# Two one-tile steps at the head of an input projection, and a load put behind the first scale pieces

## The chip, the cores and the metric

One core of a Trainium2 chip. The metric is the device time of one execution in microseconds (us), the median of the runs shown. PE (TensorE) multiplies, ACT (ScalarE) and DVE (VectorE) do elementwise work, POOL (GpSimd) and SP (SyncE) issue DMAs here.

## What is computed

One step of a hybrid decoder layer, float32, on 256 prompt positions and 8 samples (264 columns in all). What matters for this change is its head:

```python
mod = jax.nn.silu(c) @ p['w_mod'] + p['b_mod']          # w_mod: 2048 x 12288
sh_m, sc_m, gt_m, sh_f, sc_f, gt_f = split(mod, 6)
h = rmsnorm(x, p['g_mix']) * (1.0 + sc_m) + sh_m         # 2048 features
proj = h @ p['w_in']                                     # w_in: 2048 x 10256
...                                                      # three branches, gates, merge, w_out
h2 = rmsnorm(x, p['g_ffn']) * (1.0 + sc_f) + sh_f
x = x + gt_f * conv_ffn(h2)                              # 2048 x 11264, 5632 x 2048
```

To form a feature tile (128 features) of `h`, the kernel needs the root mean square of x over all features, and the scale (`sc_m`, section 1) and the shift (`sh_m`, section 0) of these features, each a sum over all 2048 inputs of `c`.

## The kernel before

Activations lie with features on the partitions, as 16 k tiles of 128 features by 264 columns. A weight W and an activation X are split into a high and a low part (`hi`, `lo`; `xh`, `xl`), and a product is three matmuls: hi·xh, hi·xl, lo·xh (`gemm_piece`). `load_w` brings a piece of a weight on SP's queue into one of three `raw` buffers; ACT copies it to `hi`, DVE subtracts to get `lo` (four buffers each). `prefetch` and `take` keep up to three pieces traced ahead of the one in use.

The first part of the input projection (12 column groups of 256 of the branches' inputs, 4 of gate b, and one of 128 for `dt`; 17 in all) runs in steps over k, since `h` becomes known k tile by k tile. `KSTEPS` lists them as (first k tile, number of tiles): (0,2), (2,2), (4,4), (8,4), (12,4). In each step all 17 groups are multiplied into PSUM (`PG`, three buffers) and read out: by ACT (a copy to `acc`) in step 0, by DVE (an addition to `acc`) in later ones. `cuts(s)` says which groups share a weight piece: 4 divided by the step's tiles, so pieces are 512 KB, some less at the cuts; `dt` is a piece of its own at the end.

The modulation of a step is computed by `mod_part` from pieces of 512 KB (128 x 1024, two per section and k tile), by `mod_load` into the seven buffers of `rm`; step 0's are issued on SP, all later ones on POOL. `mod_fin` copies the sums (`mev`, ACT), transposes them on TensorE (`modT`), adds four partial sums and the bias (DVE); then `modulate` (called by `step_h`) makes `ht`, `xh` and `xl`. `mod_gen` is the generator of a later step's modulation: it first issues loads, `depth` turns ahead, two pieces a turn, then consumes them. `mpump(n)` adds n to a credit and lets the generator run while it is at least 1; a turn costs 2 for steps of one or two tiles and 1 for four. Each group adds 0.8, or 0.4 where the next step has one tile. What is left when a step's groups end is run by `mfinish`, then `step_h`.

Before the first step, L1183 to L1233 load step 0's modulation (`load_first`), keep TensorE busy with products of zeros (`warm`), square x (`first_sq`), sum over features (`sum_tok`, TensorE) and form `rstd0` (`rstd_tok`, which ends in a product with `dg`).

A planner puts the instructions of each engine in order: among those that its own timing takes to be ready, the one traced first. `tc.high_priority()` moves a block ahead. `tc.issue_after(ins)` queues what the block traces on the engine of `ins` behind `ins`, in order of issue alone. Tiles get their buffers as they are released.

Of the kernel before, what the change touches and what calls it, by code (L numbers as in the profile page):

```python
# [13 lines left out]
AF = mybir.ActivationFunctionType  # L14
# [17 lines left out]
NFF = 44  # L32
NGA = 4
FFP = [(0, 24), (24, 20)]
KSTEPS = [(0, 2), (2, 2), (4, 4), (8, 4), (12, 4)]

# [27 lines left out]
def cuts(s):  # L66


    if s == len(KSTEPS) - 1:
        return [[g] for g in (8, 9, 10, 11, DT, 0, 1, 2, 3, 4, 5, 6, 7, *range(12, 12 + NGA))]  # L70
    n = 4 // KSTEPS[s][1]
    out = [[DT]]
# [5 lines left out]
def pack(i):  # L78
# [8 lines left out]
    wm = f("w_mod")[0]  # L87
    for s, (k0, nk) in enumerate(KSTEPS):
        w2 = wm[:, :4096].reshape(2 * nk, 8 // nk, P, 2, D)
# [10 lines left out]
    dtp[:, :16] = dt  # L100
    for s, (k0, nk) in enumerate(KSTEPS):
        r = slice(P * k0, P * (k0 + nk))
# [95 lines left out]
def build(tc, I, O):  # L198
    nc = tc.nc
    V, S, G, TE = nc.vector, nc.scalar, nc.gpsimd, nc.tensor  # L200
# [28 lines left out]
    def W(name, shape, dt=F32):  # L229
        return wp.tile(shape, dt, tag="w", name=nm(name))  # L230

    def PM(name):
        return pm.tile([P, 512], F32, tag="m", name=nm(name))

    def PG():
        return pg.tile([P, 2, 512], F32, tag="g", name=nm("pg"))
# [4 lines left out]
    def add(o, a, b, e=V):  # L241
        e.tensor_tensor(o, a, b, op=ALU.add)
# [13 lines left out]
    def act(o, a, f, **kw):  # L256
        S.activation(o, a, f, **kw)  # L257

    def mm(o, l, r, start, stop, **kw):
        TE.matmul(o, l, r, start=start, stop=stop, skip_group_check=True, **kw)  # L260

    def newest(e):

        return next(i for i in reversed(nc.cur_bb.bb.instructions) if i.engine == e.engine)


    ident = cst.tile([P, P], F32, name="ident")
# [8 lines left out]
    def pv(n, lo=0, hi=None):  # L276
        o, w = PAR_OFF[n]
        return par[:, o + lo:o + (w if hi is None else hi)]
# [25 lines left out]
    def prefetch(n=AHEAD):  # L304
        while queue and len(ahead) <= n:
            ahead.append(load_w(*queue.popleft()))
# [23 lines left out]
    mod_ps, mod_ev = {}, {}  # L330

    def mod_load(s_, nk, sec, i):

        raw = RM("rawm")
        (nc.gpsimd if s_ else nc.sync).dma_start(raw, I[f"w_m{s_}"][2 * nk * sec + i])
        return raw.rearrange("p (k n) -> p k n", k=8 // nk)

    def mod_part(sec, i, nk, raw):
        if sec not in mod_ps:
            mod_ps[sec] = PM("mod"), [0] * 4  # L340
        ps, seen = mod_ps[sec]
        for j in range(8 // nk):
            k = 8 // nk * i + j
            c = k % 4
            seen[c] += 1
            mm(ps[32 * c:32 * c + 32, :128 * nk], cs[:, k, :], raw[:, j, :], seen[c] == 1, seen[c] == KD // 4,
               tile_position=(0, 32 * c))

    def mod_fin(sec, k0, n):
        ps, _ = mod_ps.pop(sec)  # L350
        ev = W("mev", [P, 512])
        act(ev[:, :n], ps[:, :n], AF.Copy)
        mod_ev[0] = ev
        pt = PM("modT")
        nt = n // 128
        for t in range(nt):
            TE.transpose(pt[:, 128 * t:128 * t + 128], ev[:, 128 * t:128 * t + 128], ident)  # L357
        f = 16 * sec + k0
        m = mod[:, f:f + nt, :]
        V.tensor_reduce(m, pt[:, :n].rearrange("p (t g c) -> p t c g", t=nt, g=4)[:, :, :9, :],  # L360
                        axis=AX.X, op=ALU.add)
        add(m, m, pv("b_mod", f, f + nt).unsqueeze(2).to_broadcast([P, nt, 9]))
# [123 lines left out]
    def mpump(n):  # L486
        mcredit[0] += n
        while mods and mcredit[0] >= 1:
            try:
                mcredit[0] -= next(mods[0])  # L490
            except StopIteration:
                mods.popleft()
        if not mods:
            mcredit[0] = 0.0
# [9 lines left out]
    rstd0 = cst.tile([P, T], F32, name="rstd0")  # L504

    def sum_tok(pt, sqs, first, last):

        for i, sq in enumerate(sqs):
            for b, t0 in enumerate((0, 128, T - 128)):
                mm(pt[:, b:b + 1], sq[:, t0:t0 + 128], ones[:, :1], first and i == 0 and b == 0,  # L510
                   last and i == len(sqs) - 1)
        return pt
# [19 lines left out]
    def first_sq():  # L532
        sq = []
        for j in range(4):
            sq.append(Q("sq"))
            act(sq[j], x[j], AF.Square)
            if j:
                add(sq[0], sq[0], sq[j])
        h = sq[0][:, :2, :]
        add(h, h, sq[0][:, 2:, :])  # L540
        return [h[:, 0, :], h[:, 1, :]]
# [600 lines left out]

    for s_, (k0, nk) in enumerate(KSTEPS):
        o = 0
        for i, gs in enumerate(cuts(s_)):
            n = 128 if gs == [DT] else 256 * len(gs)
# [17 lines left out]
    def DEPTH(s_):  # L1164
        nk = KSTEPS[s_][1]
        return 4 * nk if s_ == 0 else (4, 4, 1)[nk // 2]

    def step_mods(s_):
        k0, nk = KSTEPS[s_]
        return mod_gen(s_, k0, nk, DEPTH(s_))  # L1170
# [10 lines left out]
    wps = PG()  # L1181
# [3 lines left out]
    def warm(n, src=None):  # L1185

        for _ in range(n):
            if src is None:
                mm(wps[:, 0, :256], wsrc[:, :128], wsrc, True, True)
            else:  # L1190
                mm(wps[:32, 0, :256], ident[:, :32], src, True, True)


    n0 = KSTEPS[0][1]
# [3 lines left out]
    def load_first(n):  # L1198
        for sec, i in first[len(got):len(got) + n]:
            got.append(mod_load(0, n0, sec, i))  # L1200

    load_first(3)
    nc.sync.dma_start(par[:, :NPAR1], I["par"][:, :NPAR1])
    load_first(3)
    pgm = lambda n: PG()[:, 0, :]
    sq0 = first_sq()
    warm(72)
    pt0 = None
    for n, (sec, i) in enumerate(first):
        if n == 0:  # L1210
            prefetch(0)
            load_first(1)
        if n == 1:
            load_first(1)
        if n == 3:
            rs0 = rstd_tok(pt0, pgm)
            scale = newest(S)
        mod_part(sec, i, n0, got[n])
        if i == 2 * n0 - 1:
            with tc.issue_after(scale), tc.high_priority():  # L1220
                if n == 3:
                    act(rstd0, rs0, AF.Copy)
                mod_fin(sec, KSTEPS[0][0], 128 * n0)
        if n == 2:
            pt0 = sum_tok(pgm("sst"), sq0, True, True)
        if n < 7:
            warm(5)
    warm(3, mod_ev[0][:, :256])
    step_h(0)
    with tc.issue_after(newest(S)), tc.issue_after(newest(V)):  # L1230
        prefetch(1)
# [3 lines left out]
    for s_, (k0, nk) in enumerate(KSTEPS):  # L1235
        nxt = None
        if s_ + 1 < NS:
            nxt = step_mods(s_ + 1)
            mods.append(nxt)
            if s_ == 0:  # L1240
                prefetch()
                mpump(DEPTH(1))
        if s_ == 1:
            nc.sync.dma_start(par[:, NPAR1:], I["par"][:, NPAR1:])
        if k0 == 4:
            fill.append(g_prep)
        if k0 == 8:
            fill.append(g_tab)
        if s_ == NS - 1:
            finish(g_tab)  # L1250
        for g, first, o in [(g, i == 0, 256 * i) for gs in cuts(s_) for i, g in enumerate(gs)]:
            ps = PG()
            if first:
                w = take()
            if g == DT:
                gemm_piece(ps, w, Xk, k0, nk, 1, True, True)
                dst, src = acc_dt, ps[:, 0, :T]
            else:
                gemm_piece(ps, w, Xk, k0, nk, 2, True, True, o)
                if g // 2 == len(acc):  # L1260
                    acc.append(Q("acc"))
                dst, src = acc[g // 2][:, 2 * (g % 2):2 * (g % 2) + 2, :], ps[:, :, :T]
            if s_ == 0:
                act(dst, src, AF.Copy)
            else:
                add(dst, dst, src)
            if s_ == NS - 1 and g >= 12:
                act(dst, dst, AF.Sigmoid)
            if s_ == NS - 1:
                if g == 11:  # L1270
                    g_gm = gen_gm(acc[5], acc[4])
                    side.append(g_gm)
                if g == DT:
                    side.append(gen_dt(acc_dt))
                if g == 5:
                    fill.append(gen_conv(acc[:3]))
            pump(0.3 * nk)
            mpump(0.8 if KSTEPS[min(s_ + 1, NS - 1)][1] > 1 else 0.8 / 2)
            if nxt and nxt not in mods:
                step_h(s_ + 1)  # L1280
                nxt = None
        if nxt:
            mfinish(nxt)
            step_h(s_ + 1)
# [124 lines left out]
    sst = {}  # L1409
# [64 lines left out]
    wps = PG()  # L1474
# [43 lines left out]
```

## Time and profile before

| | us |
|---|---|
| median of 3 runs | 1656.61 (1653.38 to 1658.26) |
| the profiled execution | 1655.27 |
| its span, first to last instruction | 1653.6 |
| PE, DVE, ACT busy in it | 1624.5, 1095.3, 798.1 |
| first projection matmul starts | 29.21 |
| mean granted clock of TensorE | 0.992 of full speed |

The span is the time from the first to the last instruction. Busy time counts matmuls whose ends are modelled, so a PE that is busy isn't at its peak. The chain of waits follows the work that ended last back from the end: at each step to what released it, or to the instruction before it on its engine.

### The profile page before, as it was taken

What the parts mean: (1) busy time and instruction counts of PE and PEld (TensorE: products, weight loads), DVE (VectorE), ACT (ScalarE), POOL (GpSimd) and SP (SyncE); (2) the same over time, 40 slices, a digit from 0 to 9 for tenths busy, and PEclk for the clock granted to TensorE, in tenths of its full rate; (3) what the DMA queues carried; (4) which work ended last, traced back from release to release, by engine and by line L of the source; (5) the groups of instructions that cost most, each with busy time, mean ns of one, the idle gap of its engine ahead of it and who ended that gap; (6) DMA issues with size and microseconds to landing.
All of it is one profiled execution on the core that took longest, in us unless ns stands there. A gap on an engine that the chain in (4) does not pass through costs nothing.

```text
span 1653.6 us, 32301 instructions
## 1 busy us (share of the span) xinstructions
PE 1624.5 (98%) x13199; PEld 1512.6 (91%) x13199; DVE 1095.3 (66%) x1969; ACT 798.1 (48%) x1167; POOL 123.7 (7%) x237
## 2 busy tenths in 40 slices
PE   8999999999999998999999999999999999999997
PEld 6788899888888898989979999999999999999996
DVE  4588898998758586554567666666454566666553
ACT  4434358434455695433345444455333455545442
POOL 1211100111011110021110000000000000000000
PEclk9999999999999999999999999999999999999998
DMA  8988964777677886589766666556555555555552
GB/s 352 349 327 291 330 198 159 294 252 270 211 278 292 291 307 226 183 316 386 282 232 211 208 231 203 167 180 192 185 182 179 181 180 189 182 179 182 182 185 94
DMA packets 107237, 385.14 MB, mean 233 GB/s; under 512 B 12224, under 2 KB 12928, under 8 KB 107088
## 3 DMA queue, kind: packets, MB, share of 16 engines
q1 hardware_dynamic: 76032, 271.18, 48.2%
q0 software_dynamic: 31056, 111.89, 18.3%
q8 instruction: 103, 1.69, 0.4%
q14 instruction: 46, 0.38, 0.1%
HBM read 374.56 MB, written 8.46 MB: 232 GB/s over the span
## 4 chain that ended last, share of the span: by engine, by line
PE 79%; issue 11%; DMA 5%; DVE 3%; ACT 1%; POOL 1%; DVEq 0%; SPq 0%; POOLq 0%; ACTq 0%
PE pg L260 73%; PE mods L260 2%; PE mod L260 2%; DMA raw<-in_w_gc 2%; DMA raw<-in_w_out 1%; POOL raws L392 1%; DVE lo L245 1%; DMA rawm<-in_w_m 1%; ACT hi L257 1%; PE ypy L260 0%; DMA csb<-csd 0%; DMA wsT<-in_wsT 0%; PE modT L357 0%; PE hst L260 0%; PE sst L260 0%
## 5 line engine op out<-in xcount | busy, mean ns | idle before, releaser
L245 DVE TENSOR_TENSOR lo<-raw,hi 128x1024 fp32r<-128x1024 f32 (+2 forms) x495 | 602.1, 1217 | 433.2 <-ACT hi L257 419.0
L257 ACT ACTIVATE hi<-raw 128x1024 fp32r<-128x1024 f32 (+2 forms) x495 | 520.6, 1053 | 706.0 <-PE pg L260 566.6
L260 PE MATMUL pg<-hh,hi 128*128 128x264 f32 x1408 | 400.1, 284 | 0.0
L260 PE MATMUL pg<-hl,hi 128*128 128x264 f32 x1408 | 399.5, 284 | 0.0
L260 PE MATMUL pg<-hh,lo 128*128 128x264 f32 x1408 | 399.2, 284 | 0.0
L260 PE MATMUL pg<-xh,hi 128*128 128x264 f32 x1296 | 376.2, 290 | 0.0
L260 PE MATMUL pg<-xl,hi 128*128 128x264 f32 x1296 | 370.4, 286 | 0.0
L260 PE MATMUL pg<-xh,lo 128*128 128x264 f32 x1296 | 369.4, 285 | 0.5 <-DVE lo L245 0.5
L260 PEld LDWEIGHTS pg<-xh,hi 128*128 128x128 f32 x1296 | 245.4, 189 | 37.3 <-issue 18.5
L260 PEld LDWEIGHTS pg<-hh,hi 128*128 128x128 f32 x1408 | 264.8, 188 | 10.1 <-issue 8.4
L260 PEld LDWEIGHTS pg<-hl,hi 128*128 128x128 f32 x1408 | 264.5, 188 | 0.0
L260 PEld LDWEIGHTS pg<-hh,lo 128*128 128x128 f32 x1408 | 264.5, 188 | 0.0
L260 PEld LDWEIGHTS pg<-xh,lo 128*128 128x128 f32 x1296 | 244.8, 189 | 1.5 <-DVE lo L245 0.7
L260 PEld LDWEIGHTS pg<-xl,hi 128*128 128x128 f32 x1296 | 244.9, 189 | 0.5 <-issue 0.5
L260 PE MATMUL pg<-fh,hi 128*128 128x264 f32 x704 | 199.7, 284 | 0.0
L260 PE MATMUL pg<-fl,hi 128*128 128x264 f32 x704 | 199.6, 284 | 0.0
L260 PE MATMUL pg<-fh,lo 128*128 128x264 f32 x704 | 199.3, 283 | 0.0
L260 PEld LDWEIGHTS pg<-fh,hi 128*128 128x128 f32 x704 | 132.3, 188 | 0.0
L260 PEld LDWEIGHTS pg<-fl,hi 128*128 128x128 f32 x704 | 132.3, 188 | 0.0
L260 PEld LDWEIGHTS pg<-fh,lo 128*128 128x128 f32 x704 | 132.3, 188 | 0.0
L392 POOL DMA_DIRECT2D raws<-in_w_mod x128 | 67.0, 529 | 558.4 <-PE mods L260 464.3
L248 DVE SCALAR_TENSOR_TENSOR fcv<-pg,par,fcv 128x255 f32<-128x255 f32 (+1 forms) x176 | 83.9, 476 | 1.0 <-ACT fcv L257 1.0
(348 smaller groups left out, 1888.7 us busy)
## 6 DMA issues: line engine op xcount, KB each, us to landing
raw<-in_w_up SPq DMA_DIRECT2D x176, 512.0 KB, 3.5
raws<-in_w_mod POOLq DMA_DIRECT2D x128, 512.0 KB, 6.9
raw<-in_w_down SPq DMA_DIRECT2D x88, 512.0 KB, 3.5
raw<-in_w_a SPq DMA_DIRECT2D x64, 512.0 KB, 5.4
rawm<-in_w_m POOLq DMA_DIRECT2D x56, 512.0 KB, 7.0
raw<-in_w_ga SPq DMA_DIRECT2D x32, 512.0 KB, 4.1
raw<-in_w_gc SPq DMA_DIRECT2D x32, 512.0 KB, 5.6
raw<-in_w_out SPq DMA_DIRECT2D x32, 512.0 KB, 6.2
```

The costliest lines, as they stand in the source:

```text
L245: e.tensor_tensor(o, a, b, op=ALU.subtract)
L248: V.scalar_tensor_tensor(o, a, s, b, op0=op0, op1=op1)
L257: S.activation(o, a, f, **kw)
L260: TE.matmul(o, l, r, start=start, stop=stop, skip_group_check=True, **kw)
L392: nc.gpsimd.dma_start(raw, I["w_mod2"][((sec - 2) * KD + kk * i) * 2 + h].rearrange("p (c n) -> p c n", c=2))
```

## The change

`KSTEPS` gets two steps of one k tile in place of the first of two tiles. Step 0's modulation is then four pieces instead of eight; all four are loaded at once. Warm-up products are 8 after each of the first three pieces instead of 5 after each of the first seven. The sum of squares is traced before the second piece's products, `rstd0` and `mod_fin` of the scale before the third's. The first loads of the next step's modulation are traced inside `tc.issue_after(landed)`, where `landed` is the TensorE instruction traced last after the second piece. A step of one tile has weight pieces of 4, 2, 4, 4 and 2 groups and `dt`: six pieces (three of 512 KB, two of 256, one of 64) where a step of two tiles had nine (eight of 512 KB, one of 128).

```diff
-KSTEPS = [(0, 2), (2, 2), (4, 4), (8, 4), (12, 4)]
+KSTEPS = [(0, 1), (1, 1), (2, 2), (4, 4), (8, 4), (12, 4)]
...
-                mm(wps[:32, 0, :256], ident[:, :32], src, True, True)
+                mm(wps[:32, 0, :128], ident[:, :32], src, True, True)
...
-    load_first(3)
+    load_first(4)
     nc.sync.dma_start(par[:, :NPAR1], I["par"][:, :NPAR1])
-    load_first(3)
...
         if n == 0:
             prefetch(0)
-            load_first(1)
         if n == 1:
-            load_first(1)
-        if n == 3:
+            pt0 = sum_tok(pgm("sst"), sq0, True, True)
+        if n == 2:
             rs0 = rstd_tok(pt0, pgm)
             scale = newest(S)
+            with tc.issue_after(scale), tc.high_priority():
+                act(rstd0, rs0, AF.Copy)
+                mod_fin(1, KSTEPS[0][0], 128 * n0)
         mod_part(sec, i, n0, got[n])
-        if i == 2 * n0 - 1:
-            with tc.issue_after(scale), tc.high_priority():
-                if n == 3:
-                    act(rstd0, rs0, AF.Copy)
-                mod_fin(sec, KSTEPS[0][0], 128 * n0)
-        if n == 2:
-            pt0 = sum_tok(pgm("sst"), sq0, True, True)
-        if n < 7:
-            warm(5)
-    warm(3, mod_ev[0][:, :256])
+        if n == 1:
+            landed = newest(TE)
+        if n < 3:
+            warm(8)
+    with tc.issue_after(scale), tc.high_priority():
+        mod_fin(0, KSTEPS[0][0], 128 * n0)
+    warm(3, mod_ev[0][:, :128])
...
-                mpump(DEPTH(1))
+                with tc.issue_after(landed):
+                    mpump(DEPTH(1))
```

## Rows read from the trace of the kernel before

**Rows 1.** the page: busy time of the engines, and the chain by engine

```profile
PE 1624.5 (98%) x13199; PEld 1512.6 (91%) x13199; DVE 1095.3 (66%) x1969; ACT 798.1 (48%) x1167; POOL 123.7 (7%) x237
...
PE 79%; issue 11%; DMA 5%; DVE 3%; ACT 1%; POOL 1%; DVEq 0%; SPq 0%; POOLq 0%; ACTq 0%
```

**Rows 2.** the chain in order of time, 0 to 64 us: start, length, what

```profile
1.81 10.23 PE pg L260 x72
...
12.67 11.99 DMA rawm<-in_w_m
...
29.28 11.03 PE pg L260 x84
...
46.37 3.92 PE pg L260 x32
...
54.42 1.00 PE mod L260 x16
```

**Rows 3.** windows of 1 us: busy (instructions) by engine, PEclk, DMA share, GB/s

```profile
23.00:24.00 1.00, 0.01 (x2) 0.00 (x0) 0.96 (x3) 0.00 (x0) 0.71 (x2) 1.00 1.02 414
...
29.00:30.00 1.00, 1.00 (x4) 0.79 (x4) 1.00 (x1) 0.36 (x1) 0.00 (x0) 0.50 1.03 416
```

**Rows 4.** waits in 29 to 60 us: engine, waited for, total us, times, longest

```profile
PEld pg L260 <- ACT hi L257: 1.2, 2, 0.8
...
PEld pg L260 <- ACT acc L257: 0.4, 1, 0.4
```

**Rows 5.** timeline: start, us, engine, operation; before the first projection matmul

```profile
26.21 2.21 PE L260 MATMUL pg<-mev,ident 128*32 128x256 f32 x6
...
27.34 0.48 DVE L248 SCALAR_TENSOR_TENSOR xl<-ht,mod,xh 128x256 fp32r<-128x256 f32 x1 [0.37 <-ACT xh L257]
...
29.21 0.81 PE L260 MATMUL pg<-xh,hi 128*128 128x264 f32 x2
```

**Rows 6.** windows of 10 us, columns as in rows 3

```profile
10.00:20.00 10.00, 10.00 (x94) 6.49 (x92) 3.71 (x10) 2.60 (x5) 1.25 (x2) 1.00 1.03 417
```

**Rows 7.** timeline of all engines, 0 to 45 us: loads and sums of squares

```profile
9.35 1.08 ACT L257 ACTIVATE sq<-x 128x1056 f32<-128x1056 f32 x1 [0.20 <-DMA x<-in_x]
...
13.08 10.16 SPq L294 DMA_DIRECT2D raw<-in_w_a  x3
...
14.32 1.40 PE L260 MATMUL pg<-ones,sq 128*128 128x1 f32 x12
14.39 0.72 POOL L335 DMA_DIRECT2D rawm<-in_w_m  x1 [12.77 <-PE mod L260]
```

**Rows 8.** groups by form (ACT 29:60, DVE 29:98 us): busy, mean ns

```profile
L257 ACT ACTIVATE hi<-raw 128x1024 fp32r<-128x1024 f32 x9 | 9.5, 1057 | 6.7 <-DMA raw<-in_w_a 4.3 <-PE pg L260 2.5
L257 ACT ACTIVATE acc<-pg 128x528 f32<-128x528 f32 x16 | 9.4, 603 | 3.3 <-PE pg L260 3.3
...
L245 DVE TENSOR_TENSOR lo<-raw,hi 128x1024 fp32r<-128x1024 f32 x19 | 23.2, 1224 | 17.4 <-ACT hi L257 17.4
L242 DVE TENSOR_TENSOR acc<-acc,pg 128x528 f32<-128x528 f32 x16 | 11.0, 700 | 7.4 <-PE pg L260 7.4
```

**Rows 9.** timeline of SP, ACT and DVE in step 0 and at its end

```profile
30.05 12.47 SPq L294 DMA_DIRECT2D raw<-in_w_a  x6
...
33.07 1.09 ACT L257 ACTIVATE acc<-pg 128x528 f32<-128x528 f32 x2
...
60.20 0.38 ACT L257 ACTIVATE accdt<-pg 128x264 f32<-128x264 f32 x1
...
38.05 1.23 DVE L245 TENSOR_TENSOR lo<-raw,hi 128x1024 fp32r<-128x1024 f32 x1 [3.63 <-ACT hi L257]
...
61.05 0.70 DVE L242 TENSOR_TENSOR acc<-acc,pg 128x528 f32<-128x528 f32 x1
```

**Rows 10.** DMA issues in 29 to 60 us: transfers, KB each, us to landing

```profile
raw<-in_w_a SPq DMA_DIRECT2D x9, 512.0 KB, 6.8
...
raw<-in_w_a SPq DMA_DIRECT2D x1, 128.0 KB, 5.0
```

## The prediction

> **What bounds the kernel now.** I read the page first: TensorE is busy 98% of the span and the chain that ended last is 79% PE [rows 1]. So the time is TensorE's work plus the stretches in which it waits or runs slowly, and a change at the start pays only through those. The chain in order of time shows one such stretch: warm-up matmuls to 12.04, then 11.99 us in which the chain is a modulation load, then a short tail, and from 29.28 us the projection's matmuls without a break that the chain shows [rows 2]. The one-microsecond windows show it in the clock: TensorE has 0.01 us of work at 23 to 24, and at 29 to 30 the granted clock is 0.50, that is 1.2 GHz [rows 3]. After 30 TensorE is fed: in 29 to 60 its weight loads wait 1.2 us for `hi` and 0.4 for evacuation [rows 4]. The reader should therefore see a prize of at most the time by which the first projection matmul (29.21) can come earlier, and a risk in the two short steps that follow.
>
> **The first matmul.** Before, its last input is the eighth piece of step 0. It lands at 24.66 [rows 2]; then comes one chain: products, `mev`, two transposes, reduction, bias, `xh`, `xl` of the first feature tile (27.34 to 27.82) and of the second, first matmul 29.21 [rows 5]. The change halves this input to four pieces. How early they land depends on what else is moving. From 10 to 20 us the DMA engines move 417 GB/s, 1.03 of their capacity [rows 6], so arrivals are a sum of bytes. The fourth square starts at 9.35 [rows 7], when c and x (2.24 MB) have come: 2.24 / 0.417 = 5.4, so the stream counts from 4.0 us, an estimate that all arrivals below use.
>
> Does the next modulation's load wait? The new `issue_after(landed)` names a TensorE instruction, and what is traced inside are loads on POOL's queue. Such a block orders only instructions of the named engine. The kernel before shows it: the second and third weight loads are traced behind an ACT and a DVE instruction of `step_h(0)` (which run after 26 us), yet SP issues them from 13.08 [rows 7]. The first of POOL's loads runs at 14.39, when the first product frees a buffer, though it is traced after all of step 0 [rows 7]. So only the seven `rm` buffers hold these loads. With four taken by step 0 instead of seven, three are free, and POOL, idle from 1.62 (14.39 less its wait of 12.77 [rows 7]), issues three loads at once, beside x. That is the case I forecast.
>
> Its arithmetic: three loads are 1.57 MB, 3.8 us of the stream, so the first piece is there at 4.0 + (2.24 + 0.52 + 1.57) / 0.417 = 14.4. Its product frees a buffer, POOL's fourth load flows from about 16.2, and SP's remaining 0.82 MB goes at half rate: the fourth piece at 20.1. Why half: before, the load issued into POOL's traffic took those 11.99 us for 512 KB. From landing to `xl` of one feature tile is 27.82 − 24.66 = 3.2 us [rows 2, 5], so 23.3. The square sums come 3.8 later than before: last `sq` at 13.1, `rstd` at about 20.5, not later than that. But the first weight piece now lies behind: 0.58 MB more at half rate, 22.9, its `hi` 1.06 [rows 8], `lo` 1.23: both there at 25.3, and the first two matmuls need only `hi`. I take 24.7. Bounds: 23.5 (the modulation chain alone) and 25.8 (the planner puts that `hi` on ACT ahead of `mev`). Gain at the first matmul: 29.2 − 24.7 = 4.5 us. If the loads were held, the fourth piece lands at 14.4 and the sum of squares sets the end: 12.65, sums 1.4, `rtk` to `dg` 1.75, product, `rstd`, `ht`, `xh`, `xl` 2.6, so 18.8 and a gain of 10.4.
>
> By the Trainium skill (DMA: Bandwidth & Descriptors, section Queues, rings and completion order) each DMA engine goes round-robin between the queue rows that have work, packet by packet. By that rule POOL's three early loads delay x and the scale pieces by up to their own 3.8 us. If instead the queue that asked first went first, SP's stream would not be delayed and the fourth piece would be there at 14.4; the 11.99 us for a load issued before POOL's speaks for the rule.
>
> **TensorE's work behind the first matmul.** Step 0 before ran from 29.2 to 60.0 (the last copy, `accdt`, starts at 60.20 [rows 9]), 30.8 us: 198 matmuls at 0.1225 (32 in 3.92 us [rows 2]), four pairs of modulation pieces at 1.00 [rows 2], transposes 0.5, some 2 us slow clock and waits. The changed kernel does the same 198 matmuls for the first two k tiles. But it also does four more pieces in this stretch, which formerly lay ahead of it: two pairs at 1.00, **+2.0**, and two more `mod_fin`, **+0.4**.
>
> **The boundaries.** Before, the last pair of step 1's pieces ran at 54.42, with three of 17 column groups left to cover the chain to `xl`. Now step 1 has two pairs, `mod_gen` counts 2 for each, and a group adds 0.4: from the credit the first pair is traced after group 13, the second after all 17. Its chain (3.2 us from the landing, less the 0.6 of the product: 2.6) stands open. Step 2 likewise: 0.8 a group, three pairs out of four inside the step, the fourth behind it. The planner can fill the gap with the next step's products whose pieces have landed. Bounds 0 and 2.6 each; I take 1.0, **+2.0** for both, because three pieces are in buffers early.
>
> **Evacuation and weights.** A group now is 6 matmuls, 0.73 us, and still ends in one PSUM read: ACT `acc` 0.603 in step 0, DVE 0.700 in step 1 [rows 8]. Four groups share one weight piece: ACT 4 × 0.603 + 1.057 = 3.5 against PE 2.9 in step 0, DVE 4 × 0.700 + 1.224 = 4.0 in step 1. Back to back these take less (two `acc` in 1.09 us at 33.07 [rows 9]: 0.5 each, 3.1), the modulation pieces give ACT and DVE another 6 us, and `lo` can run ahead. Sixteen more DVE additions are 11.2 us of an engine that is 66% busy [rows 1]. Bounds 0 and 5 us; I take **+0.5**. Warm-up matmuls are fewer (24 instead of 35 between pieces), and TensorE idles between 12.0 and 14.4; a lower clock like that before 30 us [rows 3] I expect in both kernels, so nothing is booked for it (bounds 0 and 2 us).
>
> **What else moves.** On SP the first weight piece was the thirteenth transfer and becomes the eleventh, behind `par`; its landing is in the sum above. The sums of squares go ahead of the second product on TensorE: 12 matmuls, 1.40 us [rows 7], ready at about 16.4 when nothing else is (second piece 15.7), so the product waits some 2 us, hidden by the third piece, which comes at 17.6; without that cover it would cost the chain those 2 us, inside my bound of 25.8. The tail's warm-up products halve (6 instructions, 2.21 us, now half as wide [rows 5]); they lie beside the `xh` and `xl` chain, so this is worth nothing unless modulation pieces take the room. If the wait did hold, only later modulation loads would queue behind it on POOL, and step 1's products would wait for those.
>
> **Sum.** −4.5 + 2.0 + 0.4 + 2.0 + 0.5 = +0.4 us. Everything from the third k tile on is the same code, fed at the same rate, and is shifted by it. The profiled execution took 1655.27 (span 1653.6); the median of the three runs is 1656.61, 1.3 above it. 1655.3 + 0.4 + 1.3 = 1657.0. A difference under 0.3% (5 us) counts as none, since the runs themselves spread over 1653.38 to 1658.26.
>
> **Rivals.**
> (a) *The loads are held after all.* −10.4 + 4.9 = −5.5: 1651.1. For it: the diff says so; and with three buffers POOL could be kept from them by an order I don't see. Against: the block names another engine.
> (b) *The boundaries are covered and the pieces come at 23.5.* −5.7 + 2.4 = −3.3: 1653.3. For it: TensorE may take ready modulation matmuls in any wait.
> (c) *The weights' three buffers become the bound (slower).* A k tile is now six pieces (two half size, one of 64 KB) through three `raw` buffers: two rounds per tile, four for two, where before nine pieces made three rounds for both. One round before: issued 30.05, `lo` from 38.05 to 39.28, so 9.2 us [rows 9]; landing is 6.8 for 512 KB, 5.0 for 128 KB [rows 10], so a half piece is hardly faster. At 9.2: 24.7 + 36.8 + 2.0 = 63.5, +3.5; at 10, +6.7 or 1663.3. It counts as slower from 9.6 a round. Against it: half pieces have half the `hi` and `lo`, and POOL's traffic in that round was seven loads.
>
> **Chances.** Forecast 0.50, (a) 0.18, (b) 0.12, (c) 0.20. Faster by over 0.3%: most of (a) (it lies on the limit: 0.10), a little of (b) (0.03), and of the forecast's tail (0.07): 0.20. Slower: 0.14 of (c) and 0.05 of the forecast's tail: 0.19. The rest, 0.61, is no difference. Range 1650 to 1663: from just under (a) to (c) at 10 us a round.
>
> **What would show it.** POOL's first three `rawm` issues before 5 us (in (a): after the second piece's products). First `xh,hi` matmul between 23.5 and 25.8. The third k tile's first DVE `acc` near 61 us, as step 1's first is now at 61.05 [rows 9]. Waits of `pg` weight loads for `hi`, `lo` or `acc` of 1 to 3 us in the first two steps; over 5 us for `hi` and `lo` means (c). The prediction is wrong if the first matmul comes before 20 us, or if the trace from the third k tile on differs in length by more than 2 us.

## The result and the profile after

The changed kernel takes 1665.00 us (median of 5 runs, 1661.06 to 1665.48), the kernel before 1655.66 beside it (1653.38 to 1658.26): ratio 1.0052, 95% interval 1.0037 to 1.0066. It is slower by 9 us; forecast were 1657.0 and no difference. The ratios, here and below, are computed from the single runs and need not be the quotient of the medians. The profiled execution took 1665.13 (span 1662.7, before 1653.6). Two executions far from all others, one of 2401.71 us of e6 and one of 5572.48 us of the kernel before beside e5 to e8, count in no median or ratio below.

The page's first part and its chain, to be held against [rows 1]:

```profile
PE 1625.4 (98%) x13252; PEld 1517.1 (91%) x13252; DVE 1107.0 (67%) x1998; ACT 799.2 (48%) x1173; POOL 125.7 (8%) x241
...
PE 72%; issue 14%; DMA 5%; DVE 5%; ACT 2%; POOL 2%; SPq 0%; DVEq 0%; POOLq 0%; ACTq 0%
```

TensorE's busy time is the same to 0.9 us and its share of the chain is smaller: 8.2 of the 9.1 us by which the span grew are idle time of TensorE. Slow clock hides in the busy time and is read from the windows below.

The timeline of TensorE around the first projection matmul (columns as in [rows 5]):

```profile
23.07 0.64 PE L260 MATMUL pg<-xh,hi 128*128 128x264 f32 x3
23.64 0.64 PE L260 MATMUL mod<-rawm,cs 128*32 128x128 f32 x14
24.21 0.39 PE L260 MATMUL pg<-xl,hi 128*128 128x264 f32 x1
```

The first projection matmul starts at 23.07, 6.1 us earlier than the 29.21 of [rows 5]. It is one of three products that need no `xl`; then come modulation products, and the rest of the projection runs from 24.21. The gain that the change aims at is there. But the third k tile's first addition on DVE, at 61.05 in [rows 9], is now here (timeline of DVE):

```profile
70.33 0.70 DVE L242 TENSOR_TENSOR acc<-acc,pg 128x528 f32<-128x528 f32 x1 [0.15 <-PE pg L260]
```

To see where the 9 us arise I paired the DVE additions `acc` and `accdt` of both traces, in order from the last one (72 before, the last 72 of 89 after; step 1 adds seventeen more). The shift is +9.3 us at 61 us of the kernel before, +5.1 at 100 (99.61 to 104.71), +7.1 at 148, +6.4 at 215 and +10.2 at 344 (343.72 to 353.92). The span ends +9.1. So in this pair of traces the whole loss is made before 344 us. It has two parts: some 5 us in the first two steps (of the 9.3, about 3 are modulation products of step 3 that TensorE took early and that come back by 100), and 4 to 5 us more in the middle of the projection, where both kernels have the same work.

**The first part.** The timeline of ACT in step 0 of the changed kernel:

```profile
24.79 1.06 ACT L257 ACTIVATE hi<-raw 128x1024 fp32r<-128x1024 f32 x1 [1.47 <-DMA raw<-in_w_a]
25.75 0.26 ACT L257 ACTIVATE mev<-mod 128x128 f32<-128x128 f32 x1
25.91 0.60 ACT L257 ACTIVATE acc<-pg 128x528 f32<-128x528 f32 x1
26.80 1.96 ACT L257 ACTIVATE acc<-pg 128x528 f32<-128x528 f32 x3 [0.28 <-PE pg L260]
30.86 1.06 ACT L257 ACTIVATE hi<-raw 128x1024 fp32r<-128x1024 f32 x1 [2.11 <-DMA raw<-in_w_a]
32.70 0.63 ACT L257 ACTIVATE hi<-raw 128x512 fp32r<-128x512 f32 x1 [0.78 <-DMA raw<-in_w_a]
33.23 1.09 ACT L257 ACTIVATE acc<-pg 128x528 f32<-128x528 f32 x2
```

and of TensorE's array:

```profile
30.24 0.62 PE L260 MATMUL mod<-rawm,cs 128*32 128x128 f32 x10
33.88 0.46 PE L260 MATMUL pg<-xh,hi 128*128 128x264 f32 x1 [3.01 <-ACT acc L257]
```

ACT's next instruction at 28.8 is the `hi` of the fourth weight piece, and ACT does nothing until its load lands at 30.86. The two evacuations that TensorE needs stand behind that `hi` and the fifth piece's, until 33.23, though the last product for them ended by 30.31. TensorE waits 3.01 us for the evacuation, that is for a free PSUM tile for its next group. Why the piece is late stands on the SP and POOL queues:

```profile
6.27 6.38 SPq L294 DMA_DIRECT2D raw<-in_w_a  x3
...
23.57 19.74 SPq L294 DMA_DIRECT2D raw<-in_w_a  x8
```

```profile
1.57 1.77 POOL L335 DMA_DIRECT2D rawm<-in_w_m  x3
...
24.60 0.53 POOL L335 DMA_DIRECT2D rawm<-in_w_m  x1 [0.80 <-PE mod L260]
43.52 1.05 POOL L335 DMA_DIRECT2D rawm<-in_w_m  x2 [18.40 <-PE mod L260]
```

Three pieces fill the three `raw` buffers. The fourth load is issued at 23.57, 0.03 us after the `lo` of the first piece, which frees a buffer, beside four modulation loads of 20.9 to 24.6. The fifth and sixth pieces follow at 24.64 and 27.14, as further buffers come free. Then nothing more is issued until 33.20. The transfer view of 24 to 44 us shows the engines idle (each digit is half a microsecond, in tenths of busy time):

```profile
DMA  9999999999999711100091899999600000001698
```

From 32.5 to 33.2 us both rings of buffers are held: the modulation pieces wait for TensorE, the weight pieces for ACT's `hi` and DVE's `lo`, and TensorE waits for ACT's evacuation of PSUM. What the idle time does to the clock, in windows of 1 us (columns as in [rows 3]):

```profile
32.00:33.00 1.00, 0.00 (x0) 0.00 (x0) 1.00 (x1) 0.30 (x1) 0.00 (x0) 1.00 0.05 18
33.00:34.00 1.00, 0.12 (x1) 0.12 (x2) 0.82 (x2) 1.00 (x3) 0.00 (x0) 1.00 0.00 0
34.00:35.00 1.00, 1.00 (x5) 1.00 (x6) 0.34 (x2) 1.00 (x3) 0.00 (x0) 0.52 0.81 82
35.00:36.00 1.00, 1.00 (x6) 1.00 (x6) 0.00 (x0) 0.55 (x2) 0.00 (x0) 0.50 0.96 389
36.00:37.00 1.00, 1.00 (x7) 1.00 (x6) 0.00 (x0) 0.29 (x2) 0.00 (x0) 0.50 1.12 389
37.00:38.00 1.00, 1.00 (x8) 1.00 (x8) 0.00 (x0) 0.51 (x2) 0.00 (x0) 0.77 0.91 319
```

TensorE comes back at 1.2 GHz (0.50) and needs till 37.5 for its full clock. Counting one minus the granted clock over these windows, 1.7 us are lost, beside the 3.0 idle. Another 0.7 us is idle at 25.3 to 26.1, where TensorE's transpose waits for `mev`, which runs on ACT behind the `hi` of the third piece.

Then come the boundaries. The chain in order of time (start, length, what) runs from 25 to 68 us through the modulation loads:

```profile
25.12 18.39 issue
...
43.52 4.65 DMA rawm<-in_w_m
...
49.79 10.95 issue
...
61.28 6.00 DMA rawm<-in_w_m
...
67.33 1.06 PE mod L260 x8
68.39 6.70 PE pg L260 x53
```

A step's last pieces are loaded only when the products of the step before have freed `rm` buffers, and those now run at the steps' ends (42.79, 63.59), so the pieces land just as they are wanted. TensorE is idle for 2.0 us of 42 to 50 and for 0.8 of 62 to 70.

**The second part.** Two more stretches at half clock are new, both after waits that were shorter before. Timeline of TensorE's array:

```profile
234.03 0.83 PE L260 MATMUL vss<-ones,vsq 128*128 128x1 f32 x6 [1.59 <-DVE vsq L242]
...
337.51 0.39 PE L260 MATMUL pg<-obh,hi 128*128 128x264 f32 x1 [2.20 <-ACT gate L257]
```

and the windows behind the first of them:

```profile
233.00:234.00 1.00, 0.00 (x0) 0.00 (x0) 1.00 (x4) 0.34 (x1) 0.00 (x0) 1.00 0.55 90
...
235.00:236.00 1.00, 1.00 (x8) 1.00 (x7) 0.79 (x4) 0.98 (x2) 0.00 (x0) 0.72 0.18 70
236.00:237.00 1.00, 1.00 (x7) 1.00 (x6) 0.96 (x1) 1.00 (x1) 0.00 (x0) 0.50 0.72 123
237.00:238.00 1.00, 1.00 (x6) 1.00 (x6) 0.00 (x0) 0.20 (x1) 0.00 (x0) 0.50 0.93 377
238.00:239.00 1.00, 1.00 (x7) 1.00 (x6) 0.00 (x0) 0.00 (x0) 0.00 (x0) 0.58 0.91 135
```

Before, the two waits were 0.89 us (at 227.60) and 0.74 (at 328.08), and the granted clock stayed at 1.00 behind both. Now they are 1.59 and 2.20, and it falls to 0.50 behind both. The windows lose 1.7 us at 235 and 1.7 at 337 to 342 by the clock, and the longer waits cost 0.7 and 1.5: 5.6 together, partly made up elsewhere.

### The profile page after: what moved, and what is told of

The parts are those of the page before. It is cut to its first block, busy times and chain, and to the rows that moved or that the text cites. A ratio compares the mean times of both kernels' runs of the same rounds, so it can differ in the third digit from the quotient of the medians.

```text
span 1662.7 us, 32457 instructions
## 1 busy us (share of the span) xinstructions
PE 1625.4 (98%) x13252; PEld 1517.1 (91%) x13252; DVE 1107.0 (67%) x1998; ACT 799.2 (48%) x1173; POOL 125.7 (8%) x241
## 4 chain that ended last, share of the span: by engine, by line
PE 72%; issue 14%; DMA 5%; DVE 5%; ACT 2%; POOL 2%; SPq 0%; DVEq 0%; POOLq 0%; ACTq 0%
PE pg L260 68%; PE mods L260 2%; DVE lo L245 2%; PE mod L260 1%; DMA rawm<-in_w_m 1%; POOL raws L392 1%; DMA raw<-in_w_gc 1%; DMA raw<-in_w_out 1%; DMA hst<-in_ssm 1%; ACT hi L257 1%; ACT hup L257 0%; DMA raw<-in_w_pb 0%; DMA wsT<-in_wsT 0%; ACT hst L257 0%; DVE cv L248 0%
## 5 line engine op out<-in xcount | busy, mean ns | idle before, releaser
L245 DVE TENSOR_TENSOR lo<-raw,hi 128x1024 fp32r<-128x1024 f32 x498 | 602.5, 1211 | 429.3 <-ACT hi L257 414.4
L257 ACT ACTIVATE hi<-raw 128x1024 fp32r<-128x1024 f32 x498 | 521.4, 1048 | 721.1 <-PE pg L260 562.8
L260 PEld LDWEIGHTS pg<-hh,hi 128*128 128x128 f32 x1408 | 264.7, 188 | 10.1 <-issue 8.4
```

Source lines behind the costliest of these rows:

```text
L245: e.tensor_tensor(o, a, b, op=ALU.subtract)
```

## The experiments

Each ratio is to runs of the kernel before on the same chip. Shifts and times of single instructions are read from one profiled execution of each kernel.

### The fourth buffer and the pace

Two theories for the first part: A, the three `raw` buffers (ACT at `hi`, PSUM full, half clock); B, the boundaries, where the modulation products run late. Two edits, alone and together, and the fourth buffer in the kernel before as a control.

Four raw buffers (`wsrc` goes to the work pool to make room):

```
-    rp = pool("rp", 3)
+    rp = pool("rp", 4)
...
```

> The changed kernel with four raw buffers instead of three (the warm-up zeros move to a work buffer to make room). Theory A (weights: the fourth piece of step 0 waits for a raw buffer, lands at 30.86 us, ACT stands at its hi with evacuations behind it, PSUM fills, TensorE idles 3 us and then runs 4 us at half clock): the fourth hi runs before 28 us, the idle stretch 30.9 to 33.9 and the 0.50 clock at 34 to 38 are gone, 1665 falls by 5 to 1660. Theory B (the loss lies at the two boundaries, where the next step's modulation is traced behind all groups): the stretch moves, the boundaries at 43 to 49 and 63 to 68 wait as long as now, 1665 stays within 2. Theory R (the later trace drifts: +3 us after the third k tile): no change.

Another pace of the modulation products, 0.8 a group in step 0 (was 0.4) and 1.2 in step 1 (was 0.8):

```
-            mpump(0.8 if KSTEPS[min(s_ + 1, NS - 1)][1] > 1 else 0.8 / 2)
+            mpump({0: 0.8, 1: 1.2}.get(s_, 0.8))
```

> The changed kernel with the next step's modulation traced earlier: each group of step 0 adds 0.8 instead of 0.4, of step 1 1.2 instead of 0.8, so both sections are traced by group 9 of step 0 and group 13 of step 1. Theory B: xl of the second k tile no longer ends 6 us after the last step 0 products; the gaps at 43 to 49 and 63 to 68 shrink to 2 or less each, 1665 falls by 5 to 7. Theory A: the stall at 31 to 34 and its clock remain, and 1665 stays within 2, since the products put earlier into TensorE's queue wait there for their loads.

Both edits together:

> Four raw buffers and the earlier modulation of the two runs before together. If A and B are both right and independent the gains add: 1665 falls by 10 to about 1655, as before the change. If A alone: 1660. If B alone: 1659. If the loss lies elsewhere (R): 1665.

The kernel before with the first edit only:

> The kernel before with a fourth raw buffer in the pool that the weight pieces pass through (wsrc moved into the work pool to make room), nothing of the change. Theory A (three raw buffers hurt the changed kernel's one-tile steps in particular): before is not held by them, so about 1656, within 3 us of before, and the 12.6 us that the fourth buffer gave the changed kernel are the change's own loss. Rival G (the fourth buffer helps the whole kernel, whatever the first steps are): 1640 to 1647, some 10 us under before, and the change stays a loss of 6 to 10 us with four buffers too (1652.5 against this run).

Measured (the shift at 100 us is against the kernel before with as many buffers):

| kernel | median us | ratio, 95% interval | third k tile's first add | shift at 100 us |
|---|---|---|---|---|
| changed, three buffers | 1665.00 | 1.0052 [1.0037, 1.0066] | 70.33 | +5.1 |
| e2, pace | 1663.99 | 1.0047 [1.0033, 1.0061] | 70.51 | +7.1 |
| e1, four buffers | 1652.45 | 0.9971 [0.9958, 0.9985] | 71.14 | +4.0 |
| e4, four buffers and pace | 1647.31 | 0.9945 [0.9925, 0.9966] | 65.55 | +0.8 |
| e5, before with four buffers | 1646.34 | 0.9939 [0.9920, 0.9958] | 62.41 | 0 |

Neither edit alone moves the third k tile; both together give 4.8 us of it and nearly the whole shift at 100. With the fourth buffer the `hi` of the fourth piece runs at 27.29 and the clock stays up. The windows of e1:

```profile
31.00:32.00 1.00, 0.36 (x3) 0.14 (x2) 0.20 (x1) 0.87 (x2) 0.00 (x0) 1.00 1.02 413
32.00:33.00 1.00, 0.69 (x5) 0.69 (x6) 0.49 (x2) 1.00 (x4) 0.00 (x0) 1.00 0.85 329
...
34.00:35.00 1.00, 1.00 (x11) 1.00 (x10) 0.00 (x0) 0.92 (x2) 0.00 (x0) 1.00 1.00 397
```

But what is won there is waited for at the second boundary. The timeline of TensorE in e1:

```profile
61.77 1.93 PE L260 MATMUL mod<-rawm,cs 128*32 128x512 f32 x16
66.80 1.07 PE L260 MATMUL mod<-rawm,cs 128*32 128x512 f32 x8 [3.10 <-DMA rawm<-in_w_m]
```

with the granted clock at 0.64, 0.50, 0.50 and 0.65 from 68 to 72. With the pace alone the idle time at the boundaries is nearly gone (0.6 us of 40 to 52 and 0.2 of 60 to 70, against 2.0 and 0.8 in the changed kernel), as B has it; but the stall at 31 stays (3.40 us, matmul at 33.88) and the low clock lasts until 39. With both, the transfer view of e4 for 24 to 44 us has no hole before 41:

```profile
DMA  9999999999999999989977999999999887332010
```

So A and B are both right for the first part: two limits in series, each hidden behind the other. The control went against A's own forecast (before with four buffers near 1656) and for its rival G: the fourth buffer gives the kernel before 10 us as well, and none of it in the first steps (its shift against three buffers is +1.4 at 100 and +1.5 at 344). There it removes a wait of the same kind: at 634 us TensorE waits 5.4 us for DVE's `css`, while ACT waits up to 4.7 us at a `hi` for its load, and the clock is at 0.50 to 641; in e5 the wait for `css` is 0.9 us and no window from 620 to 650 is under 0.97. TensorE is busy 24.3 us of that stretch before and 29.0 in e5, and the clock's 3.4 us come on top: some 8 of the 10 us. In the changed kernel too most of what the fourth buffer gives comes late: at 344 us e1 is only 1.8 us ahead of it (352.15 against 353.92), at the end 11.8. Only the difference from e5 to e1, 5 to 6 us (medians 1646.34 and 1652.45, ratios 0.9939 and 0.9971), is the change's. With both edits the two layouts of the steps are the same within the intervals (1647.31 and 1646.34): the change then costs nothing measurable, and still wins nothing.

### The order on ACT, and the number of pieces

Evacuations ahead of the `hi` of the fourth piece, with three buffers:

```
-    def take():
-
-        prefetch()
+    def take(n=AHEAD):
+
+        prefetch(n)
...
-                prefetch()
...
-            if first:
+            if first and s_ == 0:
+                with tc.issue_after(newest(S)):
+                    w = take(1)
+            elif first:
```

The edit does a second thing: in step 0 it keeps one piece traced ahead instead of three (`take(1)`, and no `prefetch` before the step).

> The changed kernel, with the hi of each weight piece of the first one-tile step put behind the newest evacuation on ScalarE, so that ScalarE evacuates PSUM instead of standing at the hi of the fourth piece until its load lands. Theory A (the stand at the hi leaves TensorE without PSUM from 31 to 34 us, and the low clock follows): that idle time falls under 1.5 us, the granted clock at 34 to 37 us stays near 1.0, the first accdt of the first step comes 3 to 5 us before 44.2, and the total is 1660 to 1663. Theory B (the pieces themselves come too late, the order on ScalarE doesn't matter): the idle time moves to a wait for hi and lo of the same 3 us, total 1664 to 1667.

The same with the pace of e2:

> The late hi of e6 together with the other pace of the modulation work (0.8 in the first step, 1.2 in the second). Theory A: both early stalls and the pile of modulation products at the second boundary go, without a fourth buffer: 1658 to 1661. If the early losses are later made up or given back anyway (theory R, the end is set by the drift behind 230 us): 1662 to 1667.

e6 took 1667.23, ratio 1.0053 [1.0033, 1.0073]; e8 1667.36, 1.0065 [1.0037, 1.0092]. In e6 the stand at `hi` is gone from 24 to 34 us (TensorE busy 9.47 of 10, against 6.24) and no window from 24 to 236 us is under 0.97. But 44 to 54 has 6.71 busy (8.32 in the changed kernel), with ACT waiting for loads there (up to 4.4 us); the third k tile's first add is at 74.99. TensorE's idle time is moved, as rival B has it, and A's 1660 to 1663 (1658 to 1661 for e8) did not come; e8 lies just above R's range. Whether order alone could take the stall out is not shown, since fewer pieces are traced ahead as well. The profile of e6 also has half clock from 15.1 to 21.9 and a later first matmul (26.2), so it doesn't price the stall cleanly.

Five weight pieces per one-tile step in place of six:

```
+    if KSTEPS[s][1] == 1:
+        return [[0, 1, 2, 3], [4, 5, 6, 7], [8, 9, 10, 11], [12, 13, 14, 15], [DT]]
     n = 4 // KSTEPS[s][1]
```

> The changed kernel with the weights of its one-tile steps cut into five pieces (four, four, four, four groups and dt) in place of six (four, two, four, four, two, dt): the same bytes, three raw buffers. Theory A (three raw buffers with a short second piece let the fourth piece come late, ScalarE stands at its hi, TensorE idles at 31 to 34 us and runs at half clock to 38): with twice as much work per piece behind the first one the idle time falls to 1.5 us or less and the third k tile's first add comes 2 to 4 us earlier than 70.3; total 1660 to 1663. Rival B (the boundaries and the later drift make the loss): 1664 to 1666 whatever the pieces.

> Five pieces and the pace of e2 together (0.8 in the first step, 1.2 in the second). Theory A with B (pace gives nothing while TensorE waits for PSUM, and something once it doesn't): third k tile's first add at 64 to 66, total 1656 to 1660, three raw buffers kept. If only the fourth buffer cures it: 1663 to 1666.

> Five pieces, four raw buffers and the pace together: the version with every cure. If the cures add up on top of e4 (1647.3): 1644 to 1647, equal to before with four buffers (1646.3) or below it by up to 2. If five pieces no longer matter once there are four buffers: 1646.5 to 1648.5.

e9: 1668.66, 1.0082 [1.0058, 1.0106]; e10: 1664.22, 1.0052 [1.0034, 1.0071]; e12: 1648.02, 0.9944 [0.9925, 0.9962]. With three buffers the stall stays (windows at half clock 34 to 37), so the small second piece isn't its cause; with four the time is that of e4 within the intervals. My 1660 to 1663 for e9 and 1656 to 1660 for e10 were wrong. No kernel beats e5, the kernel before with four buffers.

### The wait that the change adds

The changed kernel without it:

```
-                with tc.issue_after(landed):
-                    mpump(DEPTH(1))
+                mpump(DEPTH(1))
```

> The changed kernel without the wait of the second step's modulation loads for the second scale piece's product. By the prediction's reading the first three loads are issued before that wait and the others stand behind TensorE's products anyhow: 1665, within 3 us of the changed kernel, first loads on POOL at 1.6 us as there. If the wait costs: 1655 to 1660.

And one in which the loads are held in earnest: a POOL instruction reads the scale's `mev`, and every later load on POOL's queue is issued behind it.

```
...
+            held = cst.tile([P, 1], F32, name="held")
+            mult(held, mod_ev[0][:, :1], mod_ev[0][:, :1], e=G)
+            HOLD.append(newest(G))
...
```

> The changed kernel with a wait that does hold: POOL first multiplies one column of the copied scale sums (mev of section 1), and every load on POOL's queue is put behind that. Theory C (POOL's three early loads cost the first matmul 5 us): x lands by 9.4 again, the fourth modulation piece by 14.5, first projection matmul near 19 to 20, and 1665 falls by 4 to 5. Against it (theory D: the gain at the front is lost because step 1's pieces then come later and its boundary grows): first matmul near 20, but 1665 within 2.

e7: 1664.38, 1.0041 [1.0023, 1.0060]; the first add of the third k tile at 70.82. The added wait does nothing, as predicted. e3: 1672.61, 1.0105 [1.0075, 1.0134]. POOL's queue in e3:

```profile
17.28 0.19 POOL L248 TENSOR_TENSOR held<-mev 128x1 f32<-128x1 f32 x1 [15.66 <-ACT mev L266]
17.41 3.86 POOL L211 DMA_DIRECT2D rawm<-in_w_m  x7
```

All seven loads then go out at once, the fourth weight piece falls behind them (issued 21.87, `hi` at 29.11), and TensorE waits 5.17 us for PSUM. The first matmuls come at 21 to 22, about 2 us earlier, and the third k tile 12 us later (82.65). Theories C (4 to 5 us less) and D (within 2) were both wrong. So held in this way, all seven at once, the loads do not give the gain that rival (a) makes of it: the early loads feed the two short steps.

### Is the second part the change's own?

The kernel before, with twelve products of each of four groups of step 1 made twice into the same PSUM tile: 48 matmuls, no wait added.

```
-                gemm_piece(ps, w, Xk, k0, nk, 2, True, True, o)
+                for _ in range(2 if s_ == 1 and g in (0, 1, 6, 7) else 1):
+                    gemm_piece(ps, w, Xk, k0, nk, 2, True, True, o)
```

> The kernel before, with the 12 products of four groups of its second step made twice into the same PSUM tile (48 products more, the output the same): at 121 ns each that is 5.8 us of TensorE work with no wait added, a pure delay of about what the changed kernel has lost by 100 us. Theory R1 (a delay of that size is carried to the end and no more): 1660.5 to 1663. Theory R2 (any shift makes new waits and stretches of half clock later, as at 235 and 338 us of the changed kernel): 1664 to 1668. Rival (TensorE has slack there): under 1659.

Measured: 1663.83, ratio 1.0047 [1.0027, 1.0067], runs from 1659.66 to 1673.69; the profiled run is the longest of them (span 1671.2). In its trace the shift is exactly the 5.7 us of work from 77 to 100 us, 4.8 at 148, then +7.3 at 215, +8.8 at 231 and +10.1 at 344. The same two places fall to half clock. The windows of e11:

```profile
236.00:237.00 1.00, 1.00 (x7) 1.00 (x6) 0.79 (x3) 0.98 (x2) 0.00 (x0) 0.52 0.21 57
237.00:238.00 1.00, 1.00 (x6) 1.00 (x6) 0.83 (x1) 0.99 (x2) 0.00 (x0) 0.50 0.68 201
238.00:239.00 1.00, 1.00 (x6) 1.00 (x6) 0.00 (x0) 0.09 (x1) 0.00 (x0) 0.50 0.99 348
```

behind a wait for `vsq` of 2.49 us. A delay with no change in it grows in this profile much as the changed kernel's does, by 4.4 us at 344, and by 12 at the end. By medians the growth is less sure: 7.0 us for 5.8 of work, between the ranges of R1 and R2, and the interval (4.5 to 11.1 us) holds 5.8 too. So R2 is not shown, only possible.

Other traces speak against a simple rule. e10 has the shift (+5.4 at 100) with neither stretch at half clock, and +6.7 at 344. e4, with +2.1 at 100 and +2.6 at 148 us against the kernel before, waits 2.53 us for `vsq` and falls to half clock at 233. e7, whose first loads go out as in the changed kernel, has +5.9 at 100, no wait for `vsq` and no fall there, 2.79 us of wait and a fall at 335, +7.9 at 344, and ends +11.2. So some 5 us by 100 us are common to the traces of the changed kernel and e7; where the rest is lost differs from trace to trace, and why these waits grow stays open.

## Why the prediction was wrong

**The wait.** Right: POOL's first three loads go out at 1.57 us, and without the block nothing changes (e7).

**The first matmul.** Earlier, as forecast, but by another path: −6.1 measured for −4.5 forecast, at 23.07, 0.4 us before the lower bound of 23.5. Two errors nearly cancel, so the closeness is luck in part. The fourth modulation piece (issued at 5.06) landed 12.6 us later, at 17.65, not at 20.1; the pieces came 1.2 to 1.3 us apart, so no half rate is seen before it. But its product didn't run until after 19.91, behind the product with `dg` that the sums of squares lead to. The timeline of TensorE:

```profile
17.50 1.92 PE L260 MATMUL pg<-wsrc 128*128 128x256 bf16 x16
...
19.26 0.61 PE L260 MATMUL pg<-dg,ones 128*128 128x264 f32 x2
...
19.91 1.08 PE L260 MATMUL mod<-rawm,cs 128*32 128x128 f32 x32
```

The prediction had `rstd` at about 20.5 (it starts at 19.91) and let it set nothing. The last square starts at 12.33 (13.1 forecast, 9.35 before), after ACT waited 2.40 and 1.49 us for x, whose transfers now share the engines with POOL's. By the Trainium skill (DMA: Bandwidth & Descriptors, section Queues, rings and completion order) a DMA engine takes the queues that have work in turn, packet by packet; the trace agrees in that both queues are served at once: x was issued from 1.25 to 3.37, beside POOL's three loads (1.57 to 3.34), and its last square moved from 9.35 to 12.33. Single packets are not read here.

**The moved modulation work.** Right: TensorE makes 10.4 us of modulation products between the first matmul and the third k tile (4.3 before): 2.1 are the moved pieces (2.0 forecast), some 3 are step 3's, taken early and given back. The +0.4 for two more `mod_fin` is not measured by itself.

**The boundaries.** +2.0 forecast, 2.8 measured (2.0 and 0.8 idle). Their cause was named only as the chain behind the last pair; that the late pairs also hold the `rm` buffers of the pieces after them, so that these are loaded at 43.5 and 60.8, was not seen.

**"Evacuation and weights", +0.5 with bounds 0 and 5.** The step that failed. It compared ACT's 3.5 us with TensorE's 2.9 per piece, a balance of rates, and let `lo` run ahead. But three `raw` buffers allowed no load past the third piece before 23.57, and on ACT the `hi` stood in front of the evacuations. Measured: 3.0 us idle at 31, 0.7 at 25 to 26, and 1.7 by the clock at 34 to 38: 5.4. Rival (c) named the right resource with the wrong symptom: it looked for waits of `pg` for `hi` and `lo` over 5 us; the largest is for `acc`, 3.3. Waits, 24 to 60 us:

```profile
ACT hi L257 <- DMA raw<-in_w_a: 4.5, 4, 2.1
PEld pg L260 <- ACT acc L257: 3.3, 1, 3.3
```

The clock, with bounds 0 and 2 of its own, was booked at nothing, because a low one before 30 us was expected in both kernels; in the changed kernel that stretch comes later, among projection matmuls.

With the measured sizes the prediction's own terms give −6.1 + 2.1 + 2.8 + 5.4 = +4.2, near the +5.1 at 100 us; 0.9 is not assigned.

**"Everything from the third k tile on is shifted by it."** Also wrong: +9.3 at the third k tile, +5.1 at 100 us, +10.2 at 344. Measured from end to end that stretch is as long as before (1592.4 us after, 1592.5 before), so the prediction's own sign on its length shows nothing; but that is luck, since 4.2 us come back by 100 us and some 4 are lost again. Up to 1640 us the changed kernel's windows lose 10.2 us by the granted clock, those of the kernel before 6.8, those of e5 3.4; each also has a last stretch at half clock, which is left out (3.7, 6.1 and 6.2). In the changed kernel a gap that grew from 0.9 to 1.6 us cost more than its length.

## What to carry to other kernels

Where one engine, in the order of its queue, both prepares the next weights and evacuates PSUM, count buffers before rates: if the preparation can stand waiting for a load, every evacuation behind it stands too, and TensorE pays the idle time and then, here, the slow clock. Making a first step smaller brings the first matmul forward, but halves the work that covers each boundary and each ring of buffers; here both had to be mended together to get back to zero, and a fourth buffer without the change was worth as much (1646.34). When one fix moves nothing, try it together with the next limit before dropping it.

## What was not expected of the hardware

The granted clock fell behind idle times of TensorE as short as 1.59 us (235 us) and 2.20 us (338 us), and not behind 0.89 and 0.74 us at the same two places of the kernel before. Each of these falls lasted 3 to 4 us. The length of the idle time alone does not decide it: behind 1.27 us the clock fell (e11, at 338), behind 1.94 us at the same place it didn't (e10), nor behind 1.76 us before 13.99 in the changed kernel.
